# Storing the first group of an RMSNorm-Swish kernel in four growing pieces instead of one

## The chip, the cores and the metric

The kernel runs on one core of a Trainium2 chip. The metric is device microseconds per execution; most executions of a kernel agree within a few tenths, and some take 1 to 2 us longer. A profile of one execution accompanies each kernel; its span (first to last instruction) is about 1.3 us shorter than the measured time. The granted clock is the share of full speed that the profile shows.

## The reference

```python
x: 16 x 1024 x 512 float32, gamma: 512 ones, eps: 1e-5
rms = np.sqrt(np.mean(x ** 2, axis=-1, keepdims=True) + eps)
x_norm = x / rms * gamma
return x_norm * (1.0 / (1.0 + np.exp(-x_norm)))
```

There are 16384 rows of 512 floats: 33.55 MB to read and as much to write, with little arithmetic for each.

## The kernel before

The rows form 8 groups. In a group each of the 128 partitions holds 16 consecutive rows (32 KB), and a group is 4 MiB. The on-chip buffer is a ring of six groups, computed in place, so the load of group 6 must wait until group 0 has been stored. Loads are issued on SyncE's queue (q1 in the profile), stores on ScalarE's queue (q10). Computing goes by chunks of 4 rows per partition: ScalarE squares, VectorE sums and multiplies, GpSimd makes the reciprocal root, ScalarE applies Swish.

```python
gn = 16
loads = [(0, 0, 4), (0, 4, 4), (0, 8, 8)]        # (group, first row, rows)
loads += [(g, 0, gn) for g in range(1, G - 1)]
loads += [(G - 1, 0, 8), (G - 1, 8, 8)]
stores = [(g, 0, gn) for g in range(G - 1)]
stores += [(G - 1, 0, 8), (G - 1, 8, 8)]
ring = 6
cn = 4                                            # rows in a chunk
...
ends = [(g * gn + r + n) // cn for g, r, n in stores]   # chunks a store waits for
...
def load(i):                       # SyncE
    g, r, n = loads[i]
    for u, (h, q, m) in enumerate(stores):
        if h == g - ring and q < r + n and r < q + m and u not in stored_by_sync:
            nc.sync.wait_ge(st[u], 16)            # the store of the old content
    ...
for k in range(K + 3):             # ScalarE's program order
    if k < K:
        square(k)                                 # waits for the load of chunk k
    while stored < len(stores) and ends[stored] <= k - 2:
        store(stored); stored += 1
    if 2 <= k < K + 2:
        swish(k - 2)
```

Of the kernel before, what the change touches and what calls it, by code (L numbers as in the profile page):

```python
# [9 lines left out]
def kernel(  # L10
# [20 lines left out]
    gn = 16  # L31
    G = R // (P * gn)
# [1 line left out]
    loads = [(0, 0, 4), (0, 4, 4), (0, 8, 8)]  # L34
    loads += [(g, 0, gn) for g in range(1, G - 1)]
    loads += [(G - 1, 0, 8), (G - 1, 8, 8)]
    stores = [(g, 0, gn) for g in range(G - 1)]
    stores += [(G - 1, 0, 8), (G - 1, 8, 8)]
    ring = 6
    early = 2  # L40
    cn = 4
# [6 lines left out]
            chunks.append((g % ring * gn + c, i if c == r else None))  # L48
    K = len(chunks)

    ends = [(g * gn + r + n) // cn for g, r, n in stores]

    inv_d = 1.0 / float(D)
    eps_f = float(eps)
# [223 lines left out]
```

## Time and profile before

| | before |
|---|---|
| median of four runs (with the one added at the comparison) | 160.88 us (160.61 to 161.04) |
| span of the profiled run | 159.3 us |
| VectorE busy | 138.9 us, 87% |
| DMA engines busy, loads + stores | 50.0% + 48.9% |
| DMA packets | 3035 |
| wait of the chain for the last load | 2.07 us |
| last store: issued, landed | 152.29, 159.3 us |

The lines behind this table are in the prediction below. In the windows view the columns are: window, its length, busy us (and instructions) of VectorE, ScalarE and GpSimd, granted clock, DMA share and GB/s. A transfer packet counts wholly in the window where it starts, so short windows are rough.

The prediction and the experiments also use the trace's transfer records: one for each packet with its start, length, size and queue, and one for each DMA engine's completion write. They do not name the engine. They are not a view that prints as lines, so what I derive from them is given as numbers.

### The profile page before, as it was taken

What the parts mean: (1) busy time and instruction counts of PE and PEld (TensorE: products, weight loads), DVE (VectorE), ACT (ScalarE), POOL (GpSimd) and SP (SyncE); (2) the same over time, 40 slices, a digit from 0 to 9 for tenths busy, and PEclk for the clock granted to TensorE, in tenths of its full rate; (3) what the DMA queues carried; (4) which work ended last, traced back from release to release, by engine and by line L of the source; (5) the groups of instructions that cost most, each with busy time, mean ns of one, the idle gap of its engine ahead of it and who ended that gap; (6) DMA issues with size and microseconds to landing.
All of it is one profiled execution on the core that took longest, in us unless ns stands there. A gap on an engine that the chain in (4) does not pass through costs nothing.

```text
span 159.3 us, 436 instructions
## 1 busy us (share of the span) xinstructions
DVE 138.9 (87%) x162; ACT 125.2 (79%) x129; POOL 65.6 (41%) x71
## 2 busy tenths in 40 slices
DVE  0239999999999999999999999999999999599700
ACT  0935988888888888998888888888899887684720
POOL 2035444444455555544444445555554444355000
DMA  7999999999999999999999999999999999999996
GB/s 265 452 471 395 428 477 411 395 395 387 403 471 436 403 428 471 411 420 461 430 411 436 461 411 420 469 399 424 448 440 415 424 444 452 411 444 452 391 415 280
DMA packets 3035, 67.15 MB, mean 421 GB/s; under 512 B 468, under 2 KB 468, under 8 KB 472
## 3 DMA queue, kind: packets, MB, share of 16 engines
q1 hardware_dynamic: 1584, 33.56, 50.0%
q10 hardware_dynamic: 1448, 33.57, 48.9%
q14 instruction: 3, 0.02, 0.0%
HBM read 33.56 MB, written 33.56 MB: 421 GB/s over the span
## 4 chain that ended last, share of the span: by engine, by line
DVE 82%; DMA 5%; ACT 4%; another core or an unknown queue 1%; issue 1%; POOL 0%; ACTq 0%; POOLq 0%
DVE xb L219 52%; DVE ms L208 30%; DMA gamma<-in_gamma_dram 5%; ACT xb L178 2%; ACT sq L166 1%; DVE gamma_sb L232 0%; ACT junk L159 0%; POOL gamma L136 0%; POOL blank L135 0%; ACTq L158 0%; POOLq L59 0%
## 5 line engine op out<-in xcount | busy, mean ns | idle before, releaser
L219 DVE SCALAR_TENSOR_TENSOR xb<-xb,rstd,gamma_sb 128x512 f32<-128x512 f32 x128 | 87.7, 758 | 0.0
L178 ACT ACTIVATE xb<-xb 128x2048 f32<-128x2048 f32 x32 | 61.1, 1909 | 18.0 <-DVE xb L219 18.0
L208 DVE TENSOR_REDUCE ms<-sq 128x3 f32<-128x1536 f32 x32 | 56.4, 1763 | 8.9 <-ACT sq L166 8.9
L141 POOL TENSOR_SCALAR aeps<-ms 128x4 f32<-128x4 f32 x32 | 20.7, 648 | 77.3 <-DVE ms L208 77.3
L166 ACT ACTIVATE sq<-xb 128x1536 f32<-128x1536 f32 x32 | 45.9, 1433 | 0.0
L148 POOL TENSOR_TENSOR rstd<-aeps,neg_half 128x4 f32<-128x4 f32 x32 | 44.0, 1376 | 2.7
L159 ACT ACTIVATE junk<-xb 128x512 bf16<-128x512 f32 x32 | 19.7, 615 | 5.4 <-DMA xb<-in_x_dram 5.4
L159 ACT ACTIVATION_READ_ACCUMULATOR junk<-xb 128x1 f32 x32 | 6.0, 187 | 0.0
L194 ACT ACT_TABLE_LOAD x1 | 1.3, 1283 | 3.6 <-issue 3.6
L232 DVE LOAD_MASK_SELECT gamma_sb<-gamma x1 | 0.0, 14 | 2.5 <-DMA gamma<-in_gamma_dram 2.5
L135 POOL MEMSET blank<- 128x16 f32 x1 | 0.1, 112 | 1.5 <-POOLq L59 1.5
L232 DVE STREAM_SHUFFLE gamma_sb<-gamma 128x512 f32<-128x512 f32 x1 | 0.7, 717 | 0.0
L136 POOL MEMSET gamma<- 128x512 f32 x1 | 0.5, 525 | 0.0
L259 POOL MEMSET const-float32-0.0<- 128x1 f32 x1 | 0.1, 99 | 0.2 <-issue 0.2
L259 POOL MEMSET const-bfloat16-1.0<- 128x1 bf16 x1 | 0.1, 103 | 0.0
L259 POOL MEMSET const-uint8-127<- 128x1 uint8 x1 | 0.1, 102 | 0.0
L137 POOL MEMSET neg_half<- 128x4 f32 x1 | 0.1, 102 | 0.0
L259 POOL MEMSET const-float32-1.0<- 128x1 f32 x1 | 0.1, 99 | 0.0
## 6 DMA issues: line engine op xcount, KB each, us to landing
out_dram<-xb ACTq DMA_DIRECT2D x7, 4096.0 KB, 27.2
xb<-in_x_dram SPq DMA_DIRECT2D x6, 4096.0 KB, 48.4
xb<-in_x_dram SPq DMA_DIRECT2D x3, 2048.0 KB, 45.7
out_dram<-xb ACTq DMA_DIRECT2D x2, 2048.0 KB, 8.1
xb<-in_x_dram SPq DMA_DIRECT2D x2, 1024.0 KB, 5.8
scratch<-blank ACTq DMA_DIRECT2D x1, 8.0 KB, 7.9
gamma<-in_gamma_dram ACTq DMA_DIRECT2D x1, 8.0 KB
```

What stands on the lines that cost most here:

```text
L135: nc.gpsimd.memset(blank, 0.0).then_inc(s_blank, 1)
L136: nc.gpsimd.memset(gamma4, 0.0).then_inc(s_zero, 1)
L141: nc.gpsimd.tensor_scalar(out=aeps[:, k, :], in0=ms[:, k, :], scalar1=eps_f, scalar2=None, op0=ALU.add,),
L148: nc.gpsimd.tensor_tensor(out=rstd[:, k, :], in0=aeps[:, k, :], in1=neg_half, op=ALU.pow),
L159: acc = nc.scalar.activation(out=junk[k % 2], in_=xb[:, at + n_sq, :], func=AF.Square, scale=inv_d**0.5, accum_out=ms[:, k, n_sq : n_sq + 1],)
L166: square = nc.scalar.activation(out=sq[k % 2][:, 0:n_sq, :], in_=xb[:, at : at + n_sq, :], func=AF.Square, scale=inv_d**0.5,)
L178: nc.scalar.activation(out=rows, in_=rows, func=AF.Silu), s_norm, k + 1
L194: nc.scalar.preload_act_table_set("silu_and_others")
L208: nc.vector.tensor_reduce(out=ms[:, k, 0:n_sq], in_=sq[k % 2][:, 0:n_sq, :], op=ALU.add, axis=mybir.AxisListType.X,),
L219: ins = nc.vector.scalar_tensor_tensor(out=row, in0=row, scalar=rstd[:, k, j : j + 1], in1=gamma_sb, op0=ALU.mult, op1=ALU.mult,)
L232: nc.vector.stream_shuffle(gamma_sb, gamma4, [0] * 32), s_gld, 16
L259: nc = _bacc.Bacc("TRN2", target_bir_lowering=False, num_devices=1)
```

## The change

The intent is to start storing as soon as one chunk is ready, in small pieces that leave the loads most of the bandwidth, and grow from there.

```diff
-    stores = [(g, 0, gn) for g in range(G - 1)]
+    stores = [(0, 0, 1), (0, 1, 3), (0, 4, 4), (0, 8, 8)]
+    stores += [(g, 0, gn) for g in range(1, G - 1)]
     stores += [(G - 1, 0, 8), (G - 1, 8, 8)]
@@
-    ends = [(g * gn + r + n) // cn for g, r, n in stores]
+    ends = [-(-(g * gn + r + n) // cn) for g, r, n in stores]
```

## The prediction

> **What bounds the kernel now.** I read first the head of the page: busy shares, the slices, and the DMA queues.
>
> ```profile
> span 159.3 us, 436 instructions
> DVE 138.9 (87%) x162; ACT 125.2 (79%) x129; POOL 65.6 (41%) x71
> DMA  7999999999999999999999999999999999999996
> HBM read 33.56 MB, written 33.56 MB: 421 GB/s over the span
> q1 hardware_dynamic: 1584, 33.56, 50.0%
> q10 hardware_dynamic: 1448, 33.57, 48.9%
> ```
>
> The reader should see two candidates. VectorE is busy 87% of the span. The sixteen DMA engines are busy 98.9% of it (q1, the loads, plus q10, the stores), and no slice but the first and last falls below nine tenths. Second, the windows, to ask at what rate they move bytes (last two columns: DMA share, GB/s):
>
> ```profile
> 20.00:30.00 10.00, 10.00 (x12) 8.64 (x10) 4.23 (x5) 1.00 1.03 442
> 30.00:40.00 10.00, 10.00 (x12) 9.09 (x10) 4.52 (x5) 1.00 0.97 367
> 40.00:136.00 96.00, 96.00 (x113) 84.72 (x88) 46.07 (x46) 1.00 1.00 432
> 136.00:157.00 21.00, 12.44 (x16) 11.57 (x10) 4.74 (x5) 1.00 1.00 429
> ```
>
> Loads alone (20 to 30 us), loads with stores (40 to 136) and stores alone (136 to 157) all run at about 432 GB/s. The rate does not depend on the mix. One place is low, 30 to 40 us, where the first store starts. Third, the chain of waits and the landing times of the last three stores (group 6, then the two halves of group 7, each from a window around its issue at 136.93, 145.32 and 152.29 us):
>
> ```profile
> 132.79 1.91 ACT xb L178
> 134.70 2.07 another core or an unknown queue
> 136.77 0.02 issue
> ...
> 150.35 1.91 ACT xb L178
> ```
>
> ```profile
> out_dram<-xb ACTq DMA_DIRECT2D x1, 4096.0 KB, 12.7
> out_dram<-xb ACTq DMA_DIRECT2D x1, 2048.0 KB, 9.1
> out_dram<-xb ACTq DMA_DIRECT2D x1, 2048.0 KB, 7.0
> ```
>
> The chain runs through VectorE without a gap, then waits 2.07 us for the last load (issued 76.9, landed 136.8), and ends in the Swish at 150.35, which releases the last store. That looks like a VectorE bound, but the landings say otherwise: 136.93 + 12.7 = 149.6, 145.32 + 9.1 = 154.4, 152.29 + 7.0 = 159.3. The last two stores land 4.8 and 4.9 us apart, and 2 MiB at 432 GB/s is 4.85 us. So they run back to back, and the last one, issued at 152.29, stood behind its predecessor until about 154. **The end is set by the DMA backlog**, not by when VectorE finishes. The span is then about 1.4 us to the first packet (read from the trace's transfer records), 67.15 MB / 432 GB/s = 155.4 us of transfer, and 2.5 us for losses and the last receipt.
>
> **What the Trainium skill says.** "DMA: Bandwidth & Descriptors", section Bandwidth, Where 436 GB/s comes from: the ceiling is 435 GB/s, over sixteen ports. The trace agrees, 432. The same page, Queues, rings and completion order, Arbitration: each DMA engine takes turns between queues, a whole packet at a time. The trace agrees where the packets differ in size, at 108 to 134 us, when loads have 8 rows (16 KB a packet) and stores 16 rows (32 KB):
>
> ```profile
> q10 hardware_dynamic: 256, 7.34, 65.4%
> q1 hardware_dynamic: 255, 3.92, 35.1%
> ```
>
> Equal packets, bytes two to one. The page's Issuing engines are not separate DMA queues says that loads and stores share the same engines. The trace agrees: 50.0% and 48.9% make one full set.
>
> **The change part by part.** It removes one store of 4 MiB, released after the fourth chunk and issued at 31.17 us. It adds stores of 1, 3, 4 and 8 rows. The rounding up in `ends` releases the first two after chunk 0, whose Swish ends at 16.28 + 1.91 = 18.19 us; by their place in ScalarE's program they issue near 18.3 and 18.7. The 4 rows follow near 22.5, the 8 rows at 31.2 as now. Bytes, arithmetic and ring are unchanged.
>
> Issue cost: three more issues at 0.34 us each on ScalarE's queue. In the timeline the store at 31.17 lies beside a running 0.61 us activation and the next one starts no later than usual; ScalarE also idles 0.45 us per chunk. Cost on the path: 0.
>
> Packet cost: the transfer records give 1.213 us for a 32 KB packet, 0.611 for 16 KB, 0.309 for 8 KB, 0.084 for 2 KB. Halving a packet thus adds about 0.009 us. Each engine now carries 32 data packets for group 0 in place of 8: 24 x 0.009 = 0.21 us, and three more completion writes of 0.009. **Added: about 0.25 us**, on the DMA path, so on the end.
>
> Who moves when: estimate the first store packet at 18.3 + 4.5 = 22.8 us (now 31.17 to 35.67, the first record on q10). Taking turns with 32 KB load packets, eight rounds per piece take 8 x (1.213 + 0.084) = 10.4 us, 8 x (1.213 + 0.235) = 11.6, 8 x (1.213 + 0.309) = 12.2 and 8 x (1.213 + 0.611) = 14.6: group 0 is all out near 71.6 us, against 31.17 + 26.0 = 57.2 now. The early start thus makes the first group land **later**, because small packets give the loads the larger share. Load 6, which waits for it, is issued near 73 in place of 57. Loads 0 to 5 (25.2 MB) then have about run out: 8.9 MB by 22.8 us plus 32 rounds of 0.52 MB is 25.7 MB. The store queue holds group 1 by then (issued 48.4), so the engines stay busy. Load 6 is needed by VectorE only near 117 us, and at half rate lands near 95.
>
> The loads as a whole come earlier: group 7, in 32 rounds of (0.611 + 1.213) split between two pieces of 16 packets, lands near 124 us (95 + 29), not 136.8. The 2.07 us wait goes, and the last Swish ends 1.9 us sooner, near 150.4. What is that worth? By 125 us the engines have moved 52.7 MB in either order; with all 33.6 MB of loads done, 19.1 MB is stores, and 25.2 MB has been released. The backlog of 6.1 MB lasts 14 us, to 139; group 6 is released near 134.8, the halves of group 7 near 139 and 150.4, before the queue needs them (139, 149, 154). The engines never idle, so **VectorE's 1.9 us buys nothing**.
>
> What may be gained is the dip at 30 to 40 us. The records show that when the first 32 KB store packet enters, two load packets on each engine take together 3.5 us in place of 2.43: about 1.1 us lost once. If that is the price of the first packet of a second queue, in proportion to its size, a 2 KB packet pays almost none. If it is a buffer for the second stream that must grow to 32 KB anyway, it is paid in steps. Loads passing from 8 to 16 to 32 KB packets show no such step, which favours the first reading a little: 0.55 x 1.1 = 0.6 us.
>
> Sum: 160.99 + 0.25 - 0.6 = 160.6 us.
>
> **The rivals.** *The VectorE chain sets the end:* removing the 2.07 us wait gives about 159.1 us. For it: the chain view and a VectorE without gaps from 13.5 to 137 us. Against it: the last two stores are back to back. I give it one in ten. *The dip disappears wholly:* 160.99 - 1.1 + 0.25 = 160.1. *The dip is paid in full:* 161.2 us. *The early stores starve the first chunks or idle the engines:* if load 6 came so late that both queues emptied for the two microseconds of a receipt and an issue, 162 to 163. Against it: near 20 us VectorE works on the third chunk of group 0 while 7.7 MB (nearly two groups) have landed, and group 1's store stands ready when the loads run out. Unlikely, one in thirty.
>
> **Range and chances.** The two readings of the dip span 160.1 to 161.2; the three runs of before spread over 0.4 us; the VectorE rival takes the low edge to 159.6. Range 159.6 to 161.4. Two per cent is 3.2 us: no mechanism I found reaches it, since the bytes and the rate stand, and only 5.6 us of the 160.99 lie outside 155.4 us of transfer. Same 0.97, faster 0.015, slower 0.015.
>
> **What would show each step right or wrong.** Right: store issues near 18, 19, 22.5 and 31 us; group 0's last piece landing near 70 us; group 6's load issued after it; q1 with much the larger share from 23 to 70 us; no wait for the last load near 135 us and a last Swish near 150.4; 432 GB/s still; the last two stores still 4.9 us apart. The packet step: more store packets, with busy time up by 0.2 us or so. The dip step: the window of 20 to 30 us shows no lost bytes, or does. Wrong: an end that moves by 1.9 us with the last Swish refutes the DMA bound; a slice in the middle with DMA under nine tenths means that load 6's wait has emptied the queues; equal byte shares of the queues from 23 to 70 us would refute the turn-taking by packets.

## The result

The changed kernel took 160.26 us in the median of four runs (159.98 to 160.56), against 160.88 (160.61 to 161.04): ratio 0.9964, 95% interval 0.994 to 0.9988, "same" at the 2% threshold. A ratio here is the mean time of one kernel's runs over that of the other's of the same rounds, so it is not quite the ratio of the medians that I quote. Executions over 1.5% slower than the fastest of the same kernel are left out of the means.

The head of the page, after:

```profile
span 158.9 us, 441 instructions
DVE 139.0 (87%) x162; ACT 125.3 (79%) x129; POOL 104.8 (66%) x71
DMA  7999999999999999999999999999999999999896
DMA packets 3467, 67.15 MB, mean 423 GB/s; under 512 B 516, under 2 KB 516, under 8 KB 776
q1 hardware_dynamic: 1584, 33.56, 49.9%
q10 hardware_dynamic: 1880, 33.57, 49.2%
```

The stores have 432 more packets, and their share of the engines' time is up from 48.9 to 49.2%. The bytes are the same. The windows, after:

```profile
20.00:30.00 10.00, 10.00 (x12) 8.91 (x9) 4.09 (x4) 1.00 0.99 425
30.00:40.00 10.00, 10.00 (x13) 9.09 (x12) 4.75 (x6) 1.00 1.01 428
40.00:136.00 96.00, 96.00 (x113) 86.02 (x90) 80.52 (x44) 1.00 1.01 431
136.00:157.00 21.00, 12.12 (x16) 9.93 (x8) 9.24 (x6) 1.00 0.98 422
```

The low window at 30 to 40 us (367 GB/s before) reads 428. The long windows move at the old rate; short ones differ by a few per cent, since a packet counts where it starts. Stores by the window of their issue, after (the four pieces of group 0, then the last one of all), with us from issue to landing as last number:

```profile
out_dram<-xb ACTq DMA_DIRECT2D x1, 768.0 KB, 25.6
out_dram<-xb ACTq DMA_DIRECT2D x1, 256.0 KB, 14.4
...
out_dram<-xb ACTq DMA_DIRECT2D x1, 1024.0 KB, 34.7
...
out_dram<-xb ACTq DMA_DIRECT2D x1, 2048.0 KB, 40.7
...
out_dram<-xb ACTq DMA_DIRECT2D x1, 2048.0 KB, 7.5
```

The pieces were issued from 17.9 us on, at 22.2 and at 30.8; the last one landed at 30.84 + 40.7 = 71.5 us, where the single store had landed at 57.2. The queues from 24 to 70 us, after (packets, MB, share):

```profile
q1 hardware_dynamic: 518, 15.40, 78.7%
q10 hardware_dynamic: 525, 4.10, 21.1%
```

Equal numbers of packets, and nearly four times as many bytes for the loads. The records show the turns one by one: from 45 to 54 us, wherever a packet begins just as one single other ends, the two are of different queues (103 of 103 cases). The last chain pieces, after (start, us, what):

```profile
142.83 2.66 POOL aeps L142
145.49 0.07 issue
145.56 1.05 POOL rstd L149
146.60 0.02 issue
146.63 2.75 DVE xb L220 x4
149.38 0.02 issue
149.40 1.91 ACT xb L179
```

The wait of 2.07 us for the last load is gone: the last load landed at 124.3 us instead of 136.8. A part of what VectorE gained was lost again to a wait for GpSimd. The last store left at 151.34, 0.95 us sooner than before, and took 7.5 us to land where it had taken 7.0. The last two stores landed at 153.97 and 158.82 us, still 4.85 us apart.

### The profile page after: what moved, and what is told of

It is laid out like the page before. It is cut to its first block, busy times and chain, and to the rows that moved or that the text cites. A ratio compares the mean times of both kernels' runs of the same rounds, so it can differ in the third digit from the quotient of the medians.

```text
span 158.9 us, 441 instructions
## 1 busy us (share of the span) xinstructions
DVE 139.0 (87%) x162; ACT 125.3 (79%) x129; POOL 104.8 (66%) x71
## 3 DMA queue, kind: packets, MB, share of 16 engines
q10 hardware_dynamic: 1880, 33.57, 49.2%
## 4 chain that ended last, share of the span: by engine, by line
DVE 84%; DMA 5%; POOL 3%; ACT 1%; issue 1%; POOLq 0%
DVE xb L220 52%; DVE ms L209 32%; DMA gamma<-in_gamma_dram 5%; POOL aeps L142 2%; ACT xb L179 1%; POOL rstd L149 1%; DVE gamma_sb L233 0%; POOL gamma L137 0%; POOL blank L136 0%; POOLq L60 0%
## 5 line engine op out<-in xcount | busy, mean ns | idle before, releaser
L142 POOL TENSOR_SCALAR aeps<-ms 128x4 f32<-128x4 f32 x32 | 68.3, 2136 | 37.5 <-DVE ms L209 37.5
L220 DVE SCALAR_TENSOR_TENSOR xb<-xb,rstd,gamma_sb 128x512 f32<-128x512 f32 x128 | 88.7, 788 | 1.2 <-POOL rstd L149 1.2
L209 DVE TENSOR_REDUCE ms<-sq 128x3 f32<-128x1536 f32 x32 | 57.3, 1792 | 7.0 <-ACT sq L167 7.0
L149 POOL TENSOR_TENSOR rstd<-aeps,neg_half 128x4 f32<-128x4 f32 x32 | 35.6, 1113 | 2.7
```

Of the source, the lines that this page charges most:

```text
L142: nc.gpsimd.tensor_scalar(out=aeps[:, k, :], in0=ms[:, k, :], scalar1=eps_f, scalar2=None, op0=ALU.add,),
L149: nc.gpsimd.tensor_tensor(out=rstd[:, k, :], in0=aeps[:, k, :], in1=neg_half, op=ALU.pow),
L209: nc.vector.tensor_reduce(out=ms[:, k, 0:n_sq], in_=sq[k % 2][:, 0:n_sq, :], op=ALU.add, axis=mybir.AxisListType.X,),
L220: ins = nc.vector.scalar_tensor_tensor(out=row, in0=row, scalar=rstd[:, k, j : j + 1], in1=gamma_sb, op0=ALU.mult, op1=ALU.mult,)
```

## The experiments

Two measures recur. The **excess** is the time by which 32 KB load packets exceeded their usual 1.213 us, summed and divided by the 16 engines: what an engine lost in the mean. The **last store by engine** is when the 16 engines wrote their completion of the last store, in us after the first packet of the run: median, and how far the slowest lies behind it. The kernel before has an excess of 1.23 us in the whole profile, 1.16 of it at the opening of the store queue; the changed kernel has 0.83, and 0.00 at the opening. (The expectations use an earlier count, 1.19 and 0.77.)

### Which part of the change matters: size or time, first packet or growth

The first four runs share their runs of the kernel before (median 160.56 us).

**One row, then fifteen.**

```diff
-    stores = [(0, 0, 1), (0, 1, 3), (0, 4, 4), (0, 8, 8)]
+    stores = [(0, 0, 1), (0, 1, 15)]
```

> Group 0 in two stores, 1 row early (2 KB packets) and 15 rows (30 KB packets) at 31 us. Measure: the excess, the time that 32 KB load packets took over their usual 1.213 us, summed and divided by 16 engines, from 10 us on; before 1.19 us, the changed kernel 0.77. Growth theory (each growth of the store packet costs the loads about the time of the added bytes, so it is paid in steps): almost all of it returns between 31 and 38 us, excess 1.0 to 1.2, time as before (ratio 0.998 to 1.0). First-packet theory (only the packet that opens the second queue is dear): excess near 0.1 to 0.3, ratio about 0.993 to 0.995.

Ratio 1.0047 (1.0019 to 1.0075), median 161.18. The excess at the opening with 2 KB packets was 0.00, and 0.62 us came when the 30 KB packets entered near 35 us: neither nothing, as the first-packet theory has it, nor 1.0 to 1.2, as the growth theory has it. The window of 32 to 38 us in this kernel, and in the kernel before:

```profile
32.00:38.00 6.00, 6.00 (x9) 5.09 (x6) 3.18 (x3) 1.00 0.90 344
```

```profile
32.00:38.00 6.00, 6.00 (x9) 5.09 (x6) 3.13 (x3) 1.00 1.03 360
```

The rates of so short a window (344 and 360) do not rank the two kernels. With the bytes of each packet spread over its duration, the engines fell 0.60 us behind a steady 432 GB/s from 31 to 43 us here, and 1.12 us in the kernel before, which agrees with the excess. The time missed both theories for another reason, seen later in the same run:

```profile
130.00:135.00 5.00, 5.00 (x7) 4.29 (x5) 2.49 (x3) 1.00 1.06 459
135.00:140.00 5.00, 2.12 (x4) 1.64 (x3) 1.60 (x2) 1.00 0.77 331
```

The DMA engines idled. Group 6 was computed at 134.75 us, but its store stands behind a square of group 7 in ScalarE's program, and that waited 3.5 us for the last load, until 138.3. The store was issued at 138.44, after group 5's store had run out. So this kernel pays with an empty store queue. Idle engines were a danger that the prediction listed for the changed kernel (by another way, a late load 6); there they did not occur.

**The four pieces, held back.**

```diff
     ends = [-(-(g * gn + r + n) // cn) for g, r, n in stores]
+    ends[:4] = [4, 4, 4, 4]
```

> The same four pieces of 1, 3, 4 and 8 rows, but all held back until the fourth chunk is done (31 us), so small without early. If the packet sizes make the gain (growth or first packet): excess 0.5 to 0.9 us, ratio 0.995 to 0.998, as the changed kernel. If the early start makes the gain: as before, ratio 1.0.

Ratio 1.002 (0.9997 to 1.0044), median 160.8: by time alone this speaks for the early start, but the changed kernel itself came out at 1.0021 against nearly the same runs of before (below), so in time the two are alike, and both missed the expected 0.995 to 0.998. In the records the opening excess was 0.00 at 33 us, where the kernel before paid 1.16 at 34 us. The small first packets remove the dip, not the early start. The window of 32 to 38 us:

```profile
32.00:38.00 6.00, 6.00 (x8) 5.09 (x6) 2.71 (x3) 1.00 1.04 446
```

**Pieces of 4, 4 and 8 rows.**

```diff
-    stores = [(0, 0, 1), (0, 1, 3), (0, 4, 4), (0, 8, 8)]
+    stores = [(0, 0, 4), (0, 4, 4), (0, 8, 8)]
```

> Group 0 in 4, 4 and 8 rows: as early, but opened with 8 KB packets. Growth theory: about 0.3 us of excess at the opening, 0.3 at the step to 16 KB, and the step to 32 KB as in the changed kernel (0.26), sum 0.8 to 0.9. First-packet theory: 0.3 us at the opening and nothing after. Ratio 0.995 to 0.998 by either.

Ratio 0.9978 (0.9963 to 0.9994), median 160.22, all six runs between 159.97 and 160.49. Excess 0.29 us at the opening (8 KB), 0.33 at the step to 16 KB, 0.03 at the step to 32 KB. The sum of 0.67 is below the growth theory's 0.8 to 0.9 and above the first-packet theory's 0.3.

**Pieces of 8 and 8 rows.**

```diff
+    stores = [(0, 0, 8), (0, 8, 8)]
```

> Group 0 in two stores of 8 rows (16 KB packets), the first after the second chunk (22.5 us). Growth theory: 0.6 us of excess at the opening near 27 us, then a further 0.3 to 0.6 at the step to 32 KB. First-packet theory: 0.6 us at the opening and nothing after. Ratio 0.995 to 1.0.

Ratio 1.0037 (1.0021 to 1.0052), median 161.1, outside what I expected. The excess was 0.56 us at the opening and 0.00 at the step to 32 KB, so the dip itself behaved as the first-packet theory says. The time was lost elsewhere: its median engine finished the last store at 156.98 us, sooner than before (157.15), but its slowest 1.31 us behind that.

### What bounds the end

These runs share their runs of before with the ones above (median 160.55).

**The changed kernel again.** No edit.

> The changed kernel once more, for the spread between profiles. Ratio 0.995 to 0.998; excess of load packets from 10 us on 0.6 to 0.9 us, in steps near 54 and 85 us; last Swish ends near 151 us.

Ratio 1.0021 (0.9982 to 1.006), median 160.69, and two of six runs at 162.00 and 162.46. This missed what I expected: the gain of the first comparison did not show. The profile fell on the run of 162.00. Its excess was only 0.54 us. What it shows instead is one late engine: the median engine completed the last store at 156.53 us, sooner than in any profile of the kernel before, the slowest at 159.29, 2.76 us behind. The tail of this run:

```profile
155.00:158.00 3.00, 0.00 (x0) 0.00 (x0) 0.00 (x0) 1.00 0.82 350
158.00:160.70 2.70, 0.00 (x0) 0.00 (x0) 0.00 (x0) 1.00 0.04 18
```

In the last stretch the sixteen engines are busy 4% of the time. The records show what remains: fifteen of the sixteen completions are written by 158.3 us, and three packets of 16 KB follow one another alone, 0.61 us each. One engine is still moving its own share, and no other takes a part of it.

**Less work on VectorE.**

```diff
     def norm(k):
-        for j in range(cn):
+        for j in range(1 if k == 30 else cn):
```

> The changed kernel with three of the four normalisations of the next to last chunk left out (three rows per partition wrong on purpose): VectorE is done about 2.0 us sooner, after the last load. If the DMA backlog sets the end: ratio against before as the changed kernel, 0.995 to 0.998. If the VectorE chain sets it: 2.0 us less, ratio about 0.984.

Ratio 1.0011 (0.9985 to 1.0036), neither of the two that were expected, but near the 1.0021 of the changed kernel on the same runs of before. The last store left at 149.24 us, 1.0 us sooner than the 150.25 of the changed kernel's repeat, not 2.0, because the last chunk then had to wait for GpSimd. Those 1.0 us gave no measurable gain, against a prediction of 2.0 for a VectorE bound. (The comparison still called the output correct, presumably because with gamma of ones and an rms near 1 rows left unnormalised differ little.) Its loads and stores are those of the changed kernel, so its profile serves as a fourth reading of the excess: no excess at the opening, but 1.14 us in all, as much as in the kernel before.

**The same in the kernel before.**

> The kernel before with three of the four normalisations of the next to last chunk left out (three rows per partition wrong on purpose), 2.0 us less on VectorE after its wait for the last load. If the chain view is right and VectorE sets the end of the kernel before: 2.0 us less, ratio 0.988. If the DMA backlog sets it: 0.997 to 1.002. Its profile also gives a second reading of the opening dip: 1.0 to 1.2 us of excess between 32 and 38 us if the one reading so far was typical.

Run later, with other runs of before (median 160.74): ratio 0.9994 (0.9973 to 1.0015). By the letter this is what the DMA bound predicts, but the test did not do what it was built for. The chain of waits:

```profile
134.28 3.46 another core or an unknown queue
...
150.66 1.91 ACT xb L178
```

The last load landed 1.0 us later in this run (137.74 instead of 136.77), and the last store left at 152.60, later than the 152.29 of before. From the last load to the last store it took 14.86 us instead of 15.52, so only 0.66 us had been saved, and that was hidden by the later load. The run is inconclusive on the bound. It did give a second reading of the dip: 1.06 us at the opening.

**One MiB less to store.**

```diff
-    stores += [(g, 0, gn) for g in range(1, G - 1)]
+    stores += [(g, 0, 12 if g == 3 else gn) for g in range(1, G - 1)]
```

> The changed kernel without the last 4 rows per partition of group 3's store (1 MiB less to move, output wrong there on purpose). Pure DMA bound: 2.4 us less (1.05 MB at 432 GB/s), ratio about 0.981. VectorE bound: no change, 0.996. I expect between: the last store leaves at 151.3 us and takes about 6.9 us alone, so only 0.7 us of gain, ratio about 0.992.

The output is wrong (a part is never written). Ratio 0.9854 (0.9818 to 0.989), median 157.88. Against the changed kernel on the same runs of before (160.69) that is 2.8 us less, and against its four shorter runs (160.26 to 160.81) about 2.7. I had expected only 0.7, since VectorE would soon take over; it was the whole 2.4 us of the bytes and a little more. The last store:

```profile
out_dram<-xb ACTq DMA_DIRECT2D x1, 2048.0 KB, 6.4
```

It left at 150.20, not 151.3 as I had assumed from the first profile with its wait for GpSimd, and took 6.4 us to land, not 6.9. So it no longer queued. The slowest engine was only 0.27 us behind, after 1.22 us at the store before: the backlog had gone, and the engines that were late had caught up.

The 6.4 us also say how near the other bound was. In the kernel before, the last store left at 152.29 us; without a queue it would have landed at about 158.7, only 0.6 us before the 159.3 of the profile. In the repeats of the changed kernel (150.25 and 150.30) that estimate is 156.7 us. So the change took VectorE away from the bound, and this run, which ended at 150.20 + 6.4, is at the point where VectorE takes over.

**Both taken away.** The edits of the two runs above together.

> Both taken away, the normalisations and the 1 MiB. If the two bounds end within a microsecond of each other, the gains do not add but release each other: 2.0 to 2.4 us less than the changed kernel, ratio about 0.981 to 0.984, where the skip alone gave nothing.

Ratio 0.9863 (0.9825 to 0.9901), median 158.43; the runs were 157.60, 157.67 and 157.74, then 159.12 to 160.35. (The 160.35 counts as slow.) The ratio missed the expected 0.981 to 0.984 because of the long runs. Its three shortest runs lie 0.2 us below the three shortest of the kernel with only the bytes removed. The last store left at 149.65, 0.55 us sooner, so the test again moved VectorE less than intended. In both runs the time follows the bytes; what VectorE gains on top of that is 0.2 us here, and too small to be told from the spread.

### Is the gain real, and can it be had without the tail?

These three share their runs of before with the skip in the kernel before (median 160.74). They and that skip ran on another chip than the other experiments, so they are compared with these runs of before alone.

**The changed kernel a third time.** No edit.

> The changed kernel a third time, because the first comparison gave 0.9964 and the second 1.0021 with two of six runs above 162 us. If the gain is real and those two were a tail: most runs 160.0 to 160.6, ratio of medians about 0.998, perhaps one run in four 1 to 2 us longer. If there is no gain: runs spread evenly about those of before.

Ratio 0.9995 (0.9956 to 1.0035), median 160.61. Four runs lay at 159.97 to 160.66, one at 161.86, and one at 162.38, which counts as slow and is not in the ratio. The profile (a run of 160.66) has its median engine at 156.50 us and the slowest 1.49 us behind. In all three comparisons 4 of 16 runs of the changed kernel took over 161.8 us (one of them the run that counts as slow), and none of 27 of the kernel before did, though one took 161.77; the other 12 have a median of 160.5.

**Pieces of 4, 4 and 8 rows again.** No edit to the earlier one.

> Pieces of 4, 4 and 8 rows once more: the first time 0.9978, no run above 160.5. If the tail of the changed kernel belongs to its small pieces, none here again: ratio 0.997 to 0.999 and all runs below 160.8. If the tail is chance, one or two runs above 161.3.

Ratio 0.9968 (0.995 to 0.9986), median 160.25, all six runs between 160.17 and 160.47. Excess 0.22 us at the opening and 0.42 at the step to 16 KB. The ratio lies just below the expected 0.997 to 0.999. With both intervals below 1 and no long run in twelve, this is a version that beats the kernel before, by about 0.3%. It also lies below the changed kernel in both comparisons (0.9978 beside 1.0021, 0.9968 beside 0.9995), though those intervals overlap, and its runs spread less. Its tail, to be set beside that of the changed kernel's long run above:

```profile
155.00:158.00 3.00, 0.00 (x0) 0.00 (x0) 0.00 (x0) 1.00 0.89 382
158.00:160.70 2.70, 0.00 (x0) 0.00 (x0) 0.00 (x0) 1.00 0.00 0
```

**Halves of 8 rows for groups 1 to 6.**

```diff
-    stores += [(g, 0, gn) for g in range(1, G - 1)]
+    stores += [(g, r, 8) for g in range(1, G - 1) for r in (0, 8)]
```

> The changed kernel with the stores of groups 1 to 6 in halves of 8 rows, so that store packets never grow beyond 16 KB. Packet cost: 48 more packets on each engine at 0.009 us, 0.43 us more. Growth theory: no excess near 85 us, 0.1 to 0.5 us less. Sum about the changed kernel's time, ratio 0.998 to 1.001.

Ratio 1.0016 (0.9972 to 1.0061), median 160.59, with two runs at 162.08 and 162.45. The ratio lies just above what was expected. There was no growth beyond 16 KB while loads ran, and still 0.35 us of excess fell near 85 us. So the excess that the changed kernel's first profile showed there (0.26 us) is not the price of the step to 32 KB. The records say the same: in every kernel of four pieces with whole later stores the first 32 KB store packet starts near 70 us, just as the load queue runs empty. The excess of 80 to 93 us differs between profiles of the same four pieces, 0.01, 0.12, 0.27 and 0.53 us. Its cause is open.

The numbers of the records side by side:

| kernel | packets of group 0's stores | excess at the opening, us | at the step to 16 KB (in one case 30 KB), us | last store by engine: median + slowest, us |
|---|---|---|---|---|
| before | 32 KB | 1.16 | – | 157.15 + 0.74 |
| before, VectorE skip | 32 KB | 1.06 | – | 157.47 + 0.73 |
| 8, 8 rows | 16 KB | 0.56 | – | 156.98 + 1.31 |
| 4, 4, 8 rows | 8, 8, 16 KB | 0.29 | 0.33 | 157.01 + 0.24 |
| 4, 4, 8 rows again | 8, 8, 16 KB | 0.22 | 0.42 | 156.67 + 0.78 |
| 1, 15 rows | 2, 30 KB | 0.00 | 0.62 | 158.63 + 0.13 (queue ran empty) |
| changed | 2, 6, 8, 16 KB | 0.00 | 0.38 | 156.86 + 0.62 |
| changed again | 2, 6, 8, 16 KB | 0.00 | 0.28 | 156.53 + 2.76 |
| changed, third | 2, 6, 8, 16 KB | 0.04 | 0.21 | 156.50 + 1.49 |
| changed, held back | 2, 6, 8, 16 KB | 0.00 | 0.34 | 156.71 + 2.04 |
| changed, VectorE skip | 2, 6, 8, 16 KB | 0.00 | 0.44 | 157.22 + 0.70 |
| changed, later stores in halves | 2, 6, 8, 16 KB | 0.01 | 0.29 | 157.21 + 0.79 |

## Why the prediction was right or wrong

The time was right: 160.6 predicted, 160.26 measured, inside the range, and "same". Point by point:

- **The end is set by the DMA backlog: right.** VectorE's last result came sooner in every profile of the changed kernel, and the time did not follow it. Taking 1.05 MB out of the stores took 2.7 to 2.8 us off, where VectorE's work had not changed. The two skips support this weakly, as told above. What the prediction did not see is how near the rival was in the kernel before: 0.6 us.
- **Issue times, order and landings: right, closely.** First store issued 17.9 us (18.3 predicted), first store packet at 21.2 (22.8), group 0 out at 71.5 (71.6), load 6 issued at 71.6 (73), load 6 landed at 95.2 (95), last load at 124.3 (124). It follows from the queues taking turns packet by packet, which the records show. A part of the closeness is luck. The prediction read the first store packet of the kernel before as 35.67 us, where the records have 35.25, and the first load packet as 1.4 us, where they have 1.0. Its 4.5 us from issue to first packet was 3.3 us here, and the pieces took 50.3 us from there to the last landing, not 48.8; the two errors cancelled. One more was harmless: the first half of group 7 was issued at 143.05 us, not near 139, still before the queue needed it.
- **The wait for the last load goes and buys nothing: right in kind, not quite in size.** The last Swish ended at 151.3 us, not 150.4. The missing 0.9 us is the new wait for GpSimd, whose addition took 2.66 us at the end of that run. In the repeats, where GpSimd ran at its old pace, the Swish ended at 150.2.
- **Packet cost: right.** At the usual length of each packet size the transfers of each engine add up to 155.56 us before and 155.76 after: 0.20 us, against 0.21 predicted.
- **The dip: hedged right, both readings wrong.** The prediction put 0.6 us on two readings. The opening does cost in proportion to the packet that opens the queue (0.0, 0.25, 0.56 and 1.1 us at 2, 8, 16 and 32 KB), which is the first reading. But the later step to 16 KB costs 0.2 to 0.4 us and the jump from 2 to 30 KB 0.62, and those the first reading denies. The second reading asks for 1.0 us or more at that jump and 0.3 to 0.6 at the step from 16 to 32 KB, where 0.62 and 0.00 to 0.03 were found. In sum the excess fell from 1.15 and 1.23 us in two profiles to 0.54, 0.59 and 0.83 in three, a gain of 0.3 to 0.7, but the skip on VectorE, with the same loads and stores, had 1.14 and so no gain: 0.44 of it at the step to 16 KB and 0.53 near 85 us. That the opening is cheaper is shown; that the sum always is, is not.
- **What the sum lacked: the slowest engine.** The prediction treated sixteen engines as one. A store is complete when the last of them is, and a late one is not helped by the others (the tail of the run of 162.00 us). In the three profiles of the unaltered changed kernel the median engine finished at 156.5 to 156.9 us, against 157.15 and 157.47 before: 0.3 to 1.0 us sooner, of the size that the dip less the packet cost gives. The slowest engine lay 0.6, 1.5 and 2.8 us behind, against 0.7 before, and took the gain back in the two later profiles; the two later comparisons show no gain (1.0021, 0.9995). So the 0.6 us of the first comparison is not a dependable size, and its nearness to the 0.4 us that was forecast is in part luck.

What makes an engine fall behind in a quarter of the changed kernel's runs is not settled. In the run of 162.00 us the spread grew in two places: to 1.8 us by the end of group 0's pieces, and to 4.4 us at the store of group 1, around the time when the load queue was empty. (The kernel before also has 1.9 us at its first three stores, but it is back to 0.7 by the last.) That emptiness is new: no load packet starts for 5.8 to 7.0 us near 69 us in the three profiles, because load 6 waits for the late landing of group 0, and for at most 1.8 us in the kernel of 4, 4 and 8 rows, which has no long runs. Kernels with this pause include most of those with long runs. But the four pieces held back have the longest pause, 12.2 us, and no run above 161.53 us. Also, the kernel of 1 and 15 rows has no such pause and had one run 1.2 us above its median, and the one of 8 and 8 rows has neither a pause of that size nor 2 KB packets, and a spread of 1.3 us. Both the pause and the small packets remain as suspects; neither is shown.

## What to carry to other kernels

Here every transfer engine was busy from start to end, and an earlier start, a shorter wait and less work on VectorE moved the time by nothing that could be measured. What remained was what the engines lose: about 1.1 us when a second queue opened with 32 KB packets, and 0.2 to 0.3 when it opened with 8 KB ones. The version worth trying first is the one that gained here twice, a store queue opened with moderately small packets; still smaller ones freed the first buffer late and emptied the load queue for a while, though it is not shown that this cost time. And judge a change of a third of a per cent by several comparisons and by the slowest of the sixteen engines, not by the first median.

## What the Trainium skill lacked or had wrong

- "DMA: Bandwidth & Descriptors", Where 436 GB/s comes from: it says that for transfers between HBM and SBUF the HBM side, about 358 GB/s, binds. On this single core loads with stores ran at 432 GB/s and stores alone at 429, near the ceiling of 435 that the same section gives. The sentence lacks its condition; "HBM Reference", Specifications (TRN2), has it: a core that streams alone measures well above the share per core.
- The same page, Queues, rings and completion order, gives the packet of a turn in descriptors, typically 9 to 17, and not in bytes. Here a turn was one partition's contiguous run, of 2 to 32 KB: in the kernel before the records alternate one by one in 142 of 142 cases from 40 to 57 us. How many descriptors such a run is, they do not show.
- No page: opening a second queue beside a busy one costs each engine once, by the size of the packet that opens it: 0.0, 0.25, 0.56 and 1.1 us at 2, 8, 16 and 32 KB.
- No page says by how much the sixteen engines drift apart in a saturated run. The slowest was 0.6 to 2.8 us behind the median at the last store in three profiles of one kernel, and 0.13, 0.27 and 0.54 in three profiles whose store queue had run empty shortly before.
- "SBUF — State Buffer" states, in SBUF: two separate sides, that GpSimd and VectorE exclude each other for a whole instruction when VectorE has two inputs in SBUF and GpSimd reads SBUF. The small addition on GpSimd took 0.23 us while VectorE idled. In the kernel before and in the changed kernel's two repeats it took 0.66 us beside VectorE's multiplications, as if it waited for one of them. In the first profile of the changed kernel most took 2.65 us, and the last ended with the fourth multiplication, as if it waited for all four. The page does not tell when the one happens and when the other.
